# A hybrid decoder layer on one core: which engine issues the bias, decay, memory and copy transfers, how the second feed-forward is cut, and how its block C22 is summed

## The chip, the core and the metric

The kernel runs on one core of a Trainium2 chip. A core has five engines, each with its own instruction queue that it works through in order: TensorE (PE, matmuls and transposes), VectorE (DVE), ScalarE (ACT), GpSimd (POOL) and SyncE (SP, which only issues transfers). A DMA can be issued from SP, ACT or POOL; in the profile these issues stand on three transfer queues, q1 (from SP), q10 (from ACT) and q0 (from POOL, called software_dynamic there), and all three run on the same 16 DMA engines. The metric is the device time of one execution in microseconds.

## The reference, cut to what matters

One decoder layer on x (512 tokens, 1024 features, float32): a feed-forward, a mixer with two groups of heads, a cross-attention into a fixed memory of 256 rows, and a second feed-forward.

```python
x = x + 0.5 * swiglu(rms_norm(x, norm_ffn1_w), ffn1_w_in, ffn1_w_out)
x = x + hybrid_mixer(rms_norm(x, norm_mix_w), ...)
x = x + memory_cross_attention(rms_norm(x, norm_cross_w), rms_norm(mem, norm_mem_w), w_cq, w_ck, w_cv, w_co)
x = x + 0.5 * swiglu(rms_norm(x, norm_ffn2_w), ffn2_w_in, ffn2_w_out)
return rms_norm(x, norm_final_w)

def swiglu(h, w_in, w_out):                       # 1024 -> 2 x 2816 -> 1024
    gate, up = jnp.split(h @ w_in, 2, axis=-1)
    return (jax.nn.silu(gate) * up) @ w_out
...
logits = logits + bias[None, :, None]             # mixer: one bias row per head and distance
...
seg = la_cum[:, :, :, None] - la_cum[:, :, None, :]   # mixer: 16 scan heads, chunks of 128
decay = jnp.exp(jnp.where(causal, seg, -jnp.inf))
...
k = (mem_n @ w_ck); v = (mem_n @ w_cv)            # cross-attention, 4 heads
```

## The kernel before

Every float32 matrix product is made of three TensorE passes: each operand is split into a high part (wh, an ACT copy, line 153) and a low part (wl, a DVE subtraction, line 154), and high x high, high x low and low x high are summed in PSUM. A weight tile comes from DRAM into `wr` (six buffers, SP issues the load: `load_w` line 172, `raw_w` line 244, `fetch` line 1154) and is split into `wh` and `wl` (three buffers each).

The order is written out by hand through the class `Order`: a list of dense generators (projections) and chains (attention heads, scan groups, memory tiles, copies), which are woven together by an estimated TensorE time `od.t`. The program order that comes out is kept exactly for SP and POOL (`manual_schedule` of these two); the instructions of PE, DVE and ACT are put in order by the compiler's scheduler, with program order as priority. From then on every engine works through its own list in order and waits at each instruction for its semaphores. `with behind(ins)` puts an instruction after the named ones on the same engine.

What the change touches:

- **Bias.** `queries_keys` (line 671 on) makes q and k of one of eight attention heads and fetches `bias` (128 x 512, 256 KB) from `rel_z` in DRAM, line 676, issued by POOL. `head` reads it in `scores` (DVE, line 697, output `ec`).
- **Decay rows.** `decays` (line 813 on) broadcasts 4 x 128 numbers of `cum_d` to 128 partitions, two DMAs of 256 KB per call, line 819, issued by POOL, into the single buffers `gate` and `th`. The first calls stand in `steps` behind the write of `cum_d` (line 648); each later call stands in `group` behind the matmuls `py` that read the old rows.
- **Memory tiles.** `memory_tile` (line 934 on) loads an eighth of the memory. `memory_norm` and the first `memory_prep` (feed-forward 1, `early`) use SP and fetch all eight at the start. The second `memory_prep`, spawned by the last `out_attn` (line 768), fetches each tile by POOL just before its split into `hm` (lines 157 and 158); `memory_values` (tiles `pcv`) reads these.
- **Copies and adds.** Second feed-forward weights are block matrices in a scheme with seven products in place of eight. `block_sums_in_dram` prepares sums of weight blocks in DRAM beside the mixer: a copy (line 1138, issued by ACT, behind the last weight split) and, four jobs later, an accumulating DMA (line 1142, issued by POOL). There are 46 such jobs.
- **Thirds.** Each feed-forward's 22 tiles of hidden width go through in parts `THIRDS` of 8, 8 and 6: `ffn_quads` makes them two at a time, `out_blocks` applies the output matrix. The last part ends in `at_last`, whose ACT and DVE order is by hand: four products (`e_ps[0]`, `e_ps[1]`, `b_ps[0]`, `b_ps[1]`), after each an `update` of x, `norm` and `store`.
- **C22.** In `out_blocks` the block C22 = P5 - (b) is made by keeping a copy of `e_ps` in `p5` (ACT, line 1206), subtracting `b_ps` (DVE, line 1218, `c22`) and adding the result to x (`update`, DVE, line 1182).

Of the kernel before, what the change touches and what calls it, by code (L numbers as in the profile page):

```python
# [11 lines left out]
F32 = mybir.dt.float32  # L12
R32 = mybir.dt.float32r
AF = mybir.ActivationFunctionType
# [3 lines left out]
P = 128  # L18
# [5 lines left out]
EPS = 1e-6  # L24

NPLAIN = 6
THIRDS = ((0, 8), (8, 8), (16, 6))
NUM_BUCKETS = 32
MAX_DISTANCE = 128
RW = 640  # L30
# [68 lines left out]
def body(tc, a, dbg=None):  # L99
# [420 lines left out]
    def beside(ti):  # L520
        if ti == 1:
            od.spawn(prepare())
            od.spawn(memory_norm())
        elif ti == 2:
            od.spawn(memory_prep(hm, True))

    def fin1(o):
        st_mix.add(x[o])
# [142 lines left out]
    def queries_keys(hd):  # L671
        pq = acc("pq")
        yield from proj(pq, load_w(a["wq"][hd]), h)
        q = split("q", pq, -1.0)
        bias = s2("bias")
        nc.gpsimd.dma_start(bias, bass.AP(rel_z.tensor, rel_z.offset + hd * P * (RW + 1) + P - 1, [[RW, P], [1, T]]))
        pk = acc("pk")
        yield from proj(pk, load_w(a["wk"][hd]), h)
        kq = split("k", pk)
        od.spawn(head(hd, q, kq, bias), W["h0"])  # L680
# [84 lines left out]

    def out_attn(hg, o0, o1, prep=False):
        if prep:
            od.spawn(memory_prep(hm2, False), 0.0)
        yield lambda: all(y is not None for y in ya[4 * hg : 4 * hg + 4])
        heads = ya[4 * hg : 4 * hg + 4]  # L770
        for o in range(o0, o1):
            po = acc("pm")
            yield from proj(po, load_w(a["woa"][hg, o], 4 * P), heads)
            V.tensor_tensor(x[o], x[o], po, ALU.add)
        if o1 == KT:
            ya[4 * hg : 4 * hg + 4] = [None] * 4
# [36 lines left out]
    def decays(g, j):  # L813

        rows_of[g, j], both = [], s4(("gate", "th")[j])
        for hh in range(2):
            r = both[:, 2 * hh : 2 * hh + 2].rearrange("p a (b c) -> p (a b) c", c=P)
            hd = 4 * g + 2 * j + hh
            nc.gpsimd.dma_start(r, bass.AP(cum_d.tensor, cum_d.offset + hd * P, [[0, P], [16 * P, 4], [1, P]]))
            rows_of[g, j].append(r)  # L820

    def group(g, bt, ct, xs, zs):
# [108 lines left out]
    st_mem = Stat(MEM)  # L931
    ck, cv = [], []

    def memory_tile(k, queue):
        mk = s2("mem", shape=(P, MEM))
        queue.dma_start(mk, a["memT"][k])
        return mk

    def memory_norm():
        mem = [memory_tile(k, nc.sync) for k in range(KT)]  # L940
        for mk in mem:
            yield 2.0
            with behind(recent):
                st_mem.add(mk)
        yield 3.0
        yield from st_mem.finish(6.0)

    def memory_prep(dst, early):
        mem = [memory_tile(k, nc.sync) for k in range(KT)] if early else []
        for k in range(KT):  # L950
            mk = mem[k] if early else memory_tile(k, G)
            with behind(recent):
                dst.append(split("hm", mk, par[:, C_MEM + k : C_MEM + k + 1], True))
            yield 2.0
# [164 lines left out]


    isum = [[dram.tile([P, D], F32, name=f"isum{g}{t}") for t in range(2)] for g in range(NF // 2)]
    wsum = [[dram.tile([P, nf // 2 * T], F32, name=f"wsum{c}{t}") for t in range(4)] for c, (_, nf) in enumerate(THIRDS)]

    def block_sums_in_dram():
        jobs = []
        for c, (f0, nf) in enumerate(THIRDS):
            gs = range(f0 // 2, (f0 + nf) // 2)
            jobs += [(isum[g][0], a["f2q"][g][0], a["f2q"][g][1]) for g in gs]
            jobs += [(isum[g][1], a["f2q"][g][2], isum[g][0]) for g in gs]
            blocks, sums = a[f"f2b{c}"], wsum[c]  # L1130
            for t, (to, more) in enumerate(((blocks[B12], blocks[B11]), (blocks[B12], blocks[B22]), (blocks[B22], sums[0]), (blocks[B21], sums[2]))):
                for k in range(0, nf // 2 * T, D):
                    ks = slice(k, min(k + D, nf // 2 * T))
                    jobs.append((sums[t][:, ks], to[:, ks], more[:, ks]))
        for n in range(len(jobs) + LEAD):
            if n < len(jobs):
                with behind([i for i in recent if i.engine == mybir.EngineType.Activation]):
                    S.dma_start(jobs[n][0], jobs[n][1])
                yield 5.0
            if n >= LEAD:  # L1140
                to, _, more = jobs[n - LEAD]
                G.dma_start(to, more, accum_op=ALU.add, max_dma_last_dim=4 * D)
                yield 9.0

    def out_blocks(c, g, col4, last):


        blocks = a[f"f2b{c}"]
# [29 lines left out]
                for t in range(2):  # L1178
                    yield from some(ps[t], w, which, part, t, first)

        def update(tb, half_, src):
            V.scalar_tensor_tensor(x[4 * half_ + tb], src, col4[:, tb : tb + 1], x[4 * half_ + tb], ALU.mult, ALU.add)
            if last is not None:
                last[0](tb, half_)

        bank = [acc, aux]
# [11 lines left out]
                        yield  # L1198
        for m in both:
            yield from m  # L1200
        p5, u2 = [], []
        for t in range(2):
            S.activation(b_ps[t], a_ps[t], AF.Copy)
        for t in range(2):
            p5.append(s2("p5"))
            S.activation(p5[t], e_ps[t], AF.Copy)
        yield from product(b_ps, sums[2], S2)
        for t in range(2):
            u2.append(s2("u2"))
# [4 lines left out]
            update(t, 0, a_ps[t])  # L1214
        yield from product(b_ps, sums[1], S3)
        for t in range(2):
            c22 = s2("c22")
            V.tensor_tensor(c22, p5[t], b_ps[t], ALU.subtract)
            update(t + 2, 1, c22)
        if last is None:  # L1220
            yield from product(e_ps, blocks[B22], S4)
            for t in range(2):
# [28 lines left out]

    def ffn2():
        wq, in_sums = iter(a["f2q"]), iter(isum)
        col4, gain = None, []

        sq, root = {}, {}

        def norm(tb, n):

            xt, ss, junk = x[4 * n + tb], small("fss", 1), s2("junk")  # L1260
            S.activation(junk, xt, AF.Square, accum_out=ss)
            v = small("fv", 1, bufs=6)
            if tb not in sq:
                V.tensor_scalar(v, ss, 1.0 / D, EPS, ALU.mult, ALU.add)
            else:
                V.scalar_tensor_tensor(v, ss, 1.0 / D, sq[tb], ALU.mult, ALU.add)
            V.tensor_tensor(xt, xt, gain[n], ALU.mult)
            if tb not in sq:
                sq[tb] = v
                return  # L1270
            root[tb] = small("frr", 1)
            G.tensor_tensor(root[tb], v, mhalf[:, 0:1], ALU.pow)

        def store(tb):
            rr = root[tb]
            S.activation(x[tb], x[tb], AF.Copy, scale=rr)
            nc.sync.dma_start(a["out"][tb][:, :T], x[tb])
            if tb < 3:
                S.activation(x[4 + tb], x[4 + tb], AF.Copy, scale=rr)
            else:  # L1280
                V.tensor_scalar(x[4 + tb], x[4 + tb], rr, None, ALU.mult)
            (nc.sync if tb < 3 else S).dma_start(a["out"][tb][:, T:], x[4 + tb])

        for c, (_, nf) in enumerate(THIRDS):
            g = []
            yield from ffn_quads(xs_2, wq, st_2, nf // 2, block_tiles(g, nf // 2), BY_BLOCK, in_sums, c == 0)
            if c == 0:
                col4 = small("col4", 4, bufs=1)
                V.tensor_scalar(col4, st_2.col, 0.25, None, ALU.mult)
            at_end = c == len(THIRDS) - 1  # L1290
            if at_end:
                for n in range(2):
                    gain.append(s2("gain"))
                    G.dma_start(gain[n], a["final"][n].partition_broadcast(P))
            yield from out_blocks(c, g, col4, (norm, store) if at_end else None)

    od.add(turn(1))
    od.add(ffn2())
# [16 lines left out]
def layout(i):  # L1315
# [10 lines left out]
    for n, s in (("1", "ffn1"), ("2", "ffn2")):  # L1326
        wi = tiles(i[f"{s}_w_in"][0]).reshape(2 * NF, P, KT // 2, 2, P)
        f0 = NPLAIN if n == "1" else 0

        quads = [  # L1330
            np.stack([wi[u + f : u + f + 2, :, :, k].transpose(1, 0, 2, 3).reshape(P, D) for k in range(2) for u in (NF, 0)])
            for f in range(f0, NF, 2)
        ]
        d[f"f{n}q"] = np.stack(quads)
        if n == "1":
            d["f1i"] = wi.reshape(2, NF, P, D)[:, 2:NPLAIN].swapaxes(0, 1).copy()
        wo = i[f"{s}_w_out"][0]
        for t, (f0, nf) in enumerate(THIRDS):
            part = wo[f0 * P : (f0 + nf) * P]
            if n == "1":  # L1340
                d[f"f1o{t}"] = tiles(part)
            else:

                part = part.reshape(nf // 2, 2, P, 2, T).transpose(1, 3, 2, 0, 4)
                d[f"f2b{t}"] = np.ascontiguousarray(part).reshape(4, P, nf // 2 * T)
# [44 lines left out]
```

## Time and profile before

| | us |
|---|---|
| median of 3 runs | 1348.46 (1346.11 to 1348.67) |
| the profiled execution | 1348.15 |
| its span, first to last instruction | 1346.4 |
| DVE busy | 973.4 |
| ACT busy | 669.0 |
| POOL busy | 131.1 |
| moved by q1 (SP) / q0 (POOL) / q10 (ACT) | 150.30 / 47.79 / 23.33 MB |

The profile names a tile by its name without buffer numbers and an instruction by output <- inputs. Two names are cut short: `p` is `p5`, `c` is `c22`. A row of the timeline gives start, duration, engine, line, operation and, in brackets, how long the engine had been idle before it and what released it. A row with SPq, ACTq or POOL and DMA_DIRECT2D is the issue of a transfer, not the transfer; the time to landing stands beside it in the view of DMA issues. A row of the windows gives for each engine the busy time, then the granted TensorE clock (1.00 is full speed), the busy share of the DMA engines and GB/s.

### The profile page before, as it was taken

The page shows a single profiled execution, that of the slowest core. Times are in us where ns is not written, and L with a number is a line of the kernel's source. Part 1 is how long each engine was busy: PE and PEld are TensorE (multiplying, and loading weights), DVE is VectorE, ACT ScalarE, POOL GpSimd, SP SyncE. Part 2 cuts the span into 40 slices and gives each one's busy share as a digit, 9 for nine tenths or more (in the row PEclk, how much of TensorE's full clock was granted, in tenths as well). Part 3 has the DMA queues.
Part 4 walks back from the last instruction along what each step waited for, and adds up shares of the span by engine and source line. Part 5 has one row for each costly group of instructions (what it writes and reads, how often), then busy time and mean ns, then how long its engine had stood idle before and what let it go on. Part 6 is the DMA issues. An engine that isn't in the chain of part 4 may idle for free.

```text
span 1346.4 us, 20042 instructions
## 1 busy us (share of the span) xinstructions
PE 1312.3 (97%) x7769; PEld 1140.0 (85%) x7769; DVE 973.4 (72%) x1535; ACT 669.0 (50%) x1127; POOL 131.1 (10%) x155
## 2 busy tenths in 40 slices
PE   9999999999999899999999979999999999999996
PEld 7898998799887678877788867888889989998994
DVE  6875778487886476657867757656678876987786
ACT  6442445154544365336654536434455654655555
POOL 0000010000011110210103131020001100000001
PEclk9999999999999899999999989999999999999998
DMA  7434576455484734884359676675247866666653
GB/s 268 115 121 125 141 202 236 117 151 163 147 271 85 197 78 104 185 253 118 94 153 192 130 174 205 189 193 157 71 141 212 221 209 186 180 184 194 182 166 109
DMA packets 65695, 222.71 MB, mean 165 GB/s; under 512 B 8424, under 2 KB 10960, under 8 KB 65248
## 3 DMA queue, kind: packets, MB, share of 16 engines
q1 hardware_dynamic: 47088, 150.30, 34.3%
q0 software_dynamic: 14208, 47.79, 20.7%
q10 hardware_dynamic: 4304, 23.33, 5.3%
q8 instruction: 61, 1.00, 0.3%
q14 instruction: 34, 0.28, 0.1%
HBM read 219.24 MB, written 50.91 MB: 201 GB/s over the span
## 4 chain that ended last, share of the span: by engine, by line
PE 71%; issue 18%; DMA 4%; DVE 3%; POOL 2%; ACT 1%; POOLq 0%; SPq 0%; ACTq 0%; DVEq 0%
PE qb L238 10%; PE po L144 7%; PE qa L238 7%; PE qe L238 7%; PE pxbc L144 6%; PE pm L144 6%; PE pcq L144 3%; PE ob L1172 3%; PE pz L144 2%; PE oa L1172 2%; PE oe L1172 2%; PE pa L144 2%; PE pv L144 2%; PE pg L144 2%; PE pu L144 2%
## 5 line engine op out<-in xcount | busy, mean ns | idle before, releaser
L153 ACT ACTIVATE wh<-wr 128x1024 fp32r<-128x1024 f32 (+2 forms) x311 | 317.3, 1021 | 385.6 <-PE po L144 56.7
L154 DVE TENSOR_TENSOR wl<-wr,wh 128x1024 fp32r<-128x1024 f32 (+2 forms) x311 | 365.7, 1177 | 119.4 <-ACT wh L153 117.5
L144 PE MATMUL po<-gh,wh 128*128 128x512 f32 x176 | 68.9, 392 | 0.0
L144 PE MATMUL po<-gl,wh 128*128 128x512 f32 x176 | 68.5, 390 | 0.0
L144 PE MATMUL po<-gh,wl 128*128 128x512 f32 x176 | 68.4, 389 | 0.0
L238 PE MATMUL qa<-hmh,wl 128*128 128x256 f32 x216 | 61.2, 283 | 0.1
L238 PE MATMUL qa<-hml,wh 128*128 128x256 f32 x216 | 61.1, 283 | 0.0
L238 PE MATMUL qa<-hmh,wh 128*128 128x256 f32 x216 | 61.1, 283 | 0.0
L698 ACT ACTIVATE ec<-ec,mn 128x512 f32<-128x512 f32 (+3 forms) x64 | 35.4, 555 | 36.0 <-DVE mn L697 36.0
L144 PE MATMUL pxbc<-hnh,wh 128*128 128x512 f32 x128 | 52.4, 409 | 0.0
L144 PE MATMUL pxbc<-hnh,wl 128*128 128x512 f32 x128 | 50.4, 393 | 0.0
L144 PE MATMUL pxbc<-hnl,wh 128*128 128x512 f32 x128 | 50.1, 391 | 0.0
L238 PE MATMUL qe<-s31h,wh 128*128 128x256 f32 x152 | 43.7, 288 | 1.7 <-ACT wh L153 1.7
L238 PE MATMUL qe<-s31h,wl 128*128 128x256 f32 x152 | 43.9, 289 | 0.8 <-DVE wl L154 0.8
L504 DVE TENSOR_TENSOR upd<-po,row 128x512 f32<-128x512 f32 x24 | 16.6, 691 | 38.1 <-PE po L144 37.8
L238 PE MATMUL qe<-s31l,wh 128*128 128x256 f32 x152 | 43.5, 286 | 0.0
L238 PE MATMUL qb<-s24h,wh 128*128 128x256 f32 x152 | 43.0, 283 | 0.0
L238 PE MATMUL qb<-s31h,wl 128*128 128x256 f32 x152 | 43.0, 283 | 0.0
L238 PE MATMUL qe<-s24h,wh 128*128 128x256 f32 x152 | 43.0, 283 | 0.0
L238 PE MATMUL qe<-s24l,wh 128*128 128x256 f32 x152 | 43.0, 283 | 0.0
L238 PE MATMUL qe<-s24h,wl 128*128 128x256 f32 x152 | 43.0, 283 | 0.0
L238 PE MATMUL qb<-hmh,wh 128*128 128x256 f32 x152 | 43.0, 283 | 0.0
(448 smaller groups left out, 4103.8 us busy)
## 6 DMA issues: line engine op xcount, KB each, us to landing
wr<-in_f2q SPq DMA_DIRECT2D x44, 512.0 KB, 4.4
wr<-in_f1q SPq DMA_DIRECT2D x40, 512.0 KB, 4.1
isum<-in_f2q ACTq DMA_DIRECT2D x22, 512.0 KB, 5.3
wr<-isum SPq DMA_DIRECT2D x22, 512.0 KB, 4.4
wsum<-in_f2b ACTq DMA_DIRECT2D x20, 512.0 KB, 5.1
wr<-wsum SPq DMA_DIRECT2D x20, 512.0 KB, 4.6
wr<-in_f1q POOLq DMA_DIRECT2D x16, 512.0 KB, 6.3
wr<-in_f1o SPq DMA_DIRECT2D x16, 512.0 KB, 4.7
```

What stands on the lines that cost most here:

```text
L144: nc.tensor.matmul(out, w, x, start=start, stop=stop)
L153: S.activation(hi, src, AF.Copy),
L154: V.tensor_tensor(lo, src, hi.bitcast(F32), ALU.subtract),
L238: nc.tensor.matmul(out, a_[:, wc], b_, start=first and f == 0 and kp == 0 and j == 0, stop=kp == n - 1 and j == 2, skip_group_check=True)
L504: V.tensor_tensor(upd, po, row4, ALU.mult)
L698: S.activation(ec[:, :n], ec[:, :n], AF.Exp, bias=mn, scale=-1.0, accum_out=sm[c][:, i : i + 1])
L1172: nc.tensor.matmul(ps, a_[:, ts], b_[:, ws], start=first and k == 0 and j == 0, stop=k == n - 1 and j == 2, skip_group_check=True)
```

## The change

```diff
 THIRDS = ((0, 8), (8, 8), (16, 6))
+THIRDS2 = ((0, 6), (6, 8), (14, 8))
...
-            od.spawn(memory_prep(hm, True))
+            od.spawn(memory_prep(hm))
...
-        nc.gpsimd.dma_start(bias, bass.AP(rel_z.tensor, ...))
+        S.dma_start(bias, bass.AP(rel_z.tensor, ...))
...
-            od.spawn(memory_prep(hm2, False), 0.0)
+            od.spawn(memory_prep(hm2), 0.0)
...
-            nc.gpsimd.dma_start(r, bass.AP(cum_d.tensor, ...))
+            S.dma_start(r, bass.AP(cum_d.tensor, ...))
...
-    def memory_prep(dst, early):
-        mem = [memory_tile(k, nc.sync) for k in range(KT)] if early else []
-        for k in range(KT):
-            mk = mem[k] if early else memory_tile(k, G)
+    def memory_prep(dst):
+        mem = [memory_tile(k) for k in range(KT)]
+        for k, mk in enumerate(mem):
...
-                with behind([i for i in recent if i.engine == mybir.EngineType.Activation]):
-                    S.dma_start(jobs[n][0], jobs[n][1])
+                nc.sync.dma_start(jobs[n][0], jobs[n][1])
...
-        def update(tb, half_, src):
-            V.scalar_tensor_tensor(x[4 * half_ + tb], src, col4[:, tb : tb + 1], x[4 * half_ + tb], ALU.mult, ALU.add)
-            if last is not None:
+        def update(tb, half_, src, sign=1, done=True):
+            col = (col4 if sign > 0 else ncol4)[:, tb : tb + 1]
+            V.scalar_tensor_tensor(x[4 * half_ + tb], src, col, x[4 * half_ + tb], ALU.mult, ALU.add)
+            if last is not None and done:
                 last[0](tb, half_)
...
         for t in range(2):
-            p5.append(s2("p5"))
-            S.activation(p5[t], e_ps[t], AF.Copy)
+            update(t + 2, 1, e_ps[t], 1, False)
         yield from product(b_ps, sums[2], S2)
...
         for t in range(2):
-            c22 = s2("c22")
-            V.tensor_tensor(c22, p5[t], b_ps[t], ALU.subtract)
-            update(t + 2, 1, c22)
+            update(t + 2, 1, b_ps[t], -1)
...
+                ncol4 = small("ncol4", 4, bufs=1)
+                V.tensor_scalar(ncol4, st_2.col, -0.25, None, ALU.mult)
```

ScalarE issues the 8 bias and 16 decay transfers in place of GpSimd. SyncE issues all memory tiles, the eight of a call at its start, and the 46 copies. GpSimd keeps the 46 accumulating transfers and its other small work. The second feed-forward (`ffn2`, `block_sums_in_dram`, `wsum` and the layout of its output weights) uses `THIRDS2`, parts of 6, 8 and 8 tiles; the first keeps 8, 8, 6. C22 is added to x in two steps, first `e_ps` times the column and later `b_ps` times its negative, so that `p5` and `c22` go.

More of the change, by code (lines that the diff above doesn't have):

```diff
@@ L675, in queries_keys @@
         bias = s2("bias")
-        nc.gpsimd.dma_start(bias, bass.AP(rel_z.tensor, rel_z.offset + hd * P * (RW + 1) + P - 1, [[RW, P], [1, T]]))
+        S.dma_start(bias, bass.AP(rel_z.tensor, rel_z.offset + hd * P * (RW + 1) + P - 1, [[RW, P], [1, T]]))
         pk = acc("pk")
@@ L818, in decays @@
             hd = 4 * g + 2 * j + hh
-            nc.gpsimd.dma_start(r, bass.AP(cum_d.tensor, cum_d.offset + hd * P, [[0, P], [16 * P, 4], [1, P]]))
+            S.dma_start(r, bass.AP(cum_d.tensor, cum_d.offset + hd * P, [[0, P], [16 * P, 4], [1, P]]))
             rows_of[g, j].append(r)
@@ L932, in body, with memory_tile @@
     ck, cv = [], []
-    def memory_tile(k, queue):
+    def memory_tile(k):
         mk = s2("mem", shape=(P, MEM))
-        queue.dma_start(mk, a["memT"][k])
+        nc.sync.dma_start(mk, a["memT"][k])
         return mk
     def memory_norm():
-        mem = [memory_tile(k, nc.sync) for k in range(KT)]
+        mem = [memory_tile(k) for k in range(KT)]
         for mk in mem:
@@ L946, in memory_norm @@
         yield from st_mem.finish(6.0)
-    def memory_prep(dst, early):
-        mem = [memory_tile(k, nc.sync) for k in range(KT)] if early else []
-        for k in range(KT):
-            mk = mem[k] if early else memory_tile(k, G)
+    def memory_prep(dst):
+        mem = [memory_tile(k) for k in range(KT)]
+        for k, mk in enumerate(mem):
             with behind(recent):
@@ L1121, in body @@
     isum = [[dram.tile([P, D], F32, name=f"isum{g}{t}") for t in range(2)] for g in range(NF // 2)]
-    wsum = [[dram.tile([P, nf // 2 * T], F32, name=f"wsum{c}{t}") for t in range(4)] for c, (_, nf) in enumerate(THIRDS)]
+    wsum = [[dram.tile([P, nf // 2 * T], F32, name=f"wsum{c}{t}") for t in range(4)] for c, (_, nf) in enumerate(THIRDS2)]
     def block_sums_in_dram():
         jobs = []
-        for c, (f0, nf) in enumerate(THIRDS):
+        for c, (f0, nf) in enumerate(THIRDS2):
             gs = range(f0 // 2, (f0 + nf) // 2)
@@ L1143, in block_sums_in_dram, with out_blocks @@
                 yield 9.0
-    def out_blocks(c, g, col4, last):
+    def out_blocks(c, g, col4, ncol4, last):
         blocks = a[f"f2b{c}"]
@@ L1200, in out_blocks @@
             yield from m
-        p5, u2 = [], []
+        u2 = []
         for t in range(2):
@@ L1253, in ffn2 @@
         wq, in_sums = iter(a["f2q"]), iter(isum)
-        col4, gain = None, []
+        col4, ncol4, gain = None, None, []
         sq, root = {}, {}
@@ L1282, in store @@
             (nc.sync if tb < 3 else S).dma_start(a["out"][tb][:, T:], x[4 + tb])
-        for c, (_, nf) in enumerate(THIRDS):
+        for c, (_, nf) in enumerate(THIRDS2):
             g = []
@@ L1288, in ffn2 @@
                 col4 = small("col4", 4, bufs=1)
+                ncol4 = small("ncol4", 4, bufs=1)
                 V.tensor_scalar(col4, st_2.col, 0.25, None, ALU.mult)
-            at_end = c == len(THIRDS) - 1
+                V.tensor_scalar(ncol4, st_2.col, -0.25, None, ALU.mult)
+            at_end = c == len(THIRDS2) - 1
             if at_end:
@@ L1294, in ffn2 @@
                     G.dma_start(gain[n], a["final"][n].partition_broadcast(P))
-            yield from out_blocks(c, g, col4, (norm, store) if at_end else None)
+            yield from out_blocks(c, g, col4, ncol4, (norm, store) if at_end else None)
     od.add(turn(1))
@@ L1337, in layout @@
         wo = i[f"{s}_w_out"][0]
-        for t, (f0, nf) in enumerate(THIRDS):
+        for t, (f0, nf) in enumerate(THIRDS if n == "1" else THIRDS2):
             part = wo[f0 * P : (f0 + nf) * P]
```

## The prediction

> **What bounds the kernel now.** I read the page's first part, then TensorE's own waits, then windows around each wait. The span and the engines:
>
> ```profile
> span 1346.4 us, 20042 instructions
> PE 1312.3 (97%) x7769; PEld 1140.0 (85%) x7769; DVE 973.4 (72%) x1535; ACT 669.0 (50%) x1127; POOL 131.1 (10%) x155
> ```
>
> TensorE works for 1312.3 of 1346.4 us. The change alters no matmul (22 tiles of width go through the same products in either cut), so all there is to win lies in the 34.1 us in which it stands, and in matmuls that run at a lower clock. Its longest waits (who waited, for whom, total, times, longest):
>
> ```profile
> PE pf L144 <- ACT st L862: 5.3, 1, 5.3
> PE pt L148 <- DVE mn L697: 2.6, 1, 2.6
> ```
>
> Few and single. Windows around the first two places, and the tail:
>
> ```profile
> core 0: us, PE busy (x) PEld busy (x) DVE busy (x) ACT busy (x) POOL busy (x), PEclk, DMA share, GB/s
> 457.00:462.00 5.00, 1.13 (x8) 0.73 (x8) 3.71 (x11) 3.10 (x7) 0.00 (x0) 0.88 0.61 145
> 462.00:468.00 6.00, 6.00 (x20) 4.31 (x20) 5.25 (x16) 3.83 (x11) 0.00 (x0) 0.54 0.41 123
> 795.00:803.00 8.00, 1.24 (x5) 0.60 (x3) 2.63 (x6) 2.81 (x5) 1.09 (x2) 0.73 0.74 200
> 803.00:809.00 6.00, 6.00 (x17) 4.85 (x18) 5.97 (x10) 4.89 (x12) 0.00 (x0) 0.51 0.13 38
> 1334.00:1346.40 12.40, 0.00 (x0) 0.00 (x0) 4.10 (x9) 5.17 (x11) 2.79 (x3) 0.66 0.45 169
> ```
>
> A stall costs twice. At 457 TensorE stands for 5.00 - 1.13 = 3.87 us, and in the next 6 us it is busy throughout at a mean granted clock of 0.54, which loses 6.00 x 0.46 = 2.76 us: **6.6 us**. At 795 it stands for 8.00 - 1.24 = 6.76 us and then loses 6.00 x 0.49 = 2.94 us: **9.7 us**. The tail, 12.4 us without a matmul, is the third place.
>
> **What causes the two stalls.** The first, in the timelines of POOL and DVE:
>
> ```profile
> 438.00 1.03 POOL L756 TENSOR_TENSOR rr<-ev,mhalf 128x4 f32<-128x4 f32 x1 [9.36 <-DVE ev L754]
> 439.00 0.93 POOL L1142 DMA_DIRECT2D isum<-in_f2q  x1
> 439.64 0.88 POOL L676 DMA_DIRECT2D bias<-rel_z  x1
> ```
>
> ```profile
> 457.25 0.69 DVE L697 CUSTOM_DVE_ANT_0 ec<-ps,bias 128x512 f32<-128x512 f32 x1 [9.26 <-DMA bias<-rel_z]
> ```
>
> POOL stood at line 756, let an add go first and the bias behind it; DVE then waited 9.26 us for the bias, and TensorE, which needs DVE's `mn`, stood for 3.87 of them. So TensorE has about 9.26 - 3.87 = 5.4 us of cover there. The second, in the timelines of POOL and ACT:
>
> ```profile
> 785.56 0.93 POOL L1142 DMA_DIRECT2D wsum<-in_f2b  x1
> 786.20 0.89 POOL L936 DMA_DIRECT2D mem<-in_memT  x1
> ```
>
> ```profile
> 799.83 0.51 ACT L157 ACTIVATE hm<-mem,par 128x256 fp32r<-128x256 f32 x1 [10.35 <-DMA mem<-in_memT]
> ```
>
> The first memory tile is issued behind an add as well and lands 799.8 - 786.2 = 13.6 us later. ACT stands in its list at the split `hm` for 10.35 us; behind it is the copy `st` that TensorE's `pf` needs. The tile is wanted much later, by `pcv`: the stall comes from the order in ACT's queue.
>
> **The change, part by part.**
>
> *Memory tiles to SP, eight at once.* Prices of both ways, over the whole run (issues, KB each, median us to landing):
>
> ```profile
> mem<-in_memT SPq DMA_DIRECT2D x16, 128.0 KB, 4.5
> ...
> mem<-in_memT POOLq DMA_DIRECT2D x8, 128.0 KB, 11.1
> ```
>
> SP issues in program order and as far ahead as its six `wr` buffers allow. The new tiles stand between the loads of the last `woa` and the first `wcv`. The view of the load line puts the last `woa` issue at 749.2 us (last number but the count):
>
> ```profile
> L172 SPq DMA_DIRECT2D wr<-in_woa x16: 327/328/328, 468.6 to 749.2; - x16
> ...
> DMA to landing us min/median/max: 2.5/4.7/27.7
> ```
>
> Issued from about 749 on, eight tiles of 4.5 us, even one after the other, land by 785, before ACT reaches `hm` at 799.83 - 10.35 = 789.5, and even the longest landing of that line, 27.7 us, would do for a tile (777). The stall goes: **-9.7 us**. What is late next? On DVE, busy for only 2.63 of the 8 us, the low halves of `hm` have room. If SP must wait for free small buffers, the term falls to 0.
>
> *Bias to ACT.* The row that speaks for it comes from the view of DMA issues between 436 and 458 us:
>
> ```profile
> bias<-rel_z POOLq DMA_DIRECT2D x2, 256.0 KB, 19.4
> ...
> wr<-in_wxbc SPq DMA_DIRECT2D x1, 512.0 KB, 17.2
> wsum<-in_f2b ACTq DMA_DIRECT2D x1, 512.0 KB, 9.8
> ```
>
> In this crowded stretch POOL's transfers of 256 KB took 19.4 us, one of twice the size on ACT's queue 9.8. On ACT the bias is no longer behind adds, but it is behind the first four decay transfers, which also move there. I take 9.8 us. Issued near 440.5, it lands near 450; DVE was free at 457.25 - 9.26 = 448, so it waits 2 to 3 us, within the 5.4 us of cover: **-6.6 us**. Bounds: 0, if it lands later than about 457 as now, and -6.6.
>
> [...]
>
> *Decay rows to ACT.* Off the path: no compute engine waits for them now. They leave POOL's queue, ahead of `rr` and the adds. In ACT's list they add waits, for the write of `cum_d` (issued by POOL) and six times for `py`. Queued behind such an issue are ACT's weight splits `wh`, and for those TensorE waits, with three buffers of splits as cover. How long POOL stood at these two kinds of issue:
>
> ```profile
>   PE ps L144: 58.6, 2
> ```
>
> ```profile
>   PE py L144: 99.2, 6
> ```
>
> POOL reached them far too early, since its list holds little else. ACT reaches them through its own work, which the scheduler has put in an order by its estimate. Bounds per issue: 0, and the mean of the longer kind, 58.6 / 2 = 29.3 us, less the cover. The nearest row for an engine with a full list is ACT's own, 10.35 us at `hm`; it took a transfer queued behind another. I take 0, because `py` and `ps` are matmuls that end before ACT's next inputs come, and hold the rest for a rival.
>
> *Copies to SP; issue costs.* An issue on ACT (ns, in the middle the median):
>
> ```profile
> L1138 ACTq DMA_DIRECT2D wsum<-in_f2b x24: 497/498/610, 445.3 to 991.2; - x24
> ```
>
> At 0.50 us per issue ACT loses 46 x 0.50 = 23 us and gains 24 x 0.50 = 12; at the 0.33 us of the load rows SP gains 46 x 0.33 = 15 us in 1346. Neither is near its limit. On SP's queue a copy stands ahead of weight loads and delays them by its transfer. No TensorE wait is due to a load even where landing took 17.2 us, since loads run up to six buffers ahead; cost 0, bounded above by one stall of the second kind, 9.7. POOL keeps the adds, and its waits no longer hold anything else.
>
> *Thirds of 6, 8, 8 and C22 in two steps.* Inside, the boundaries now have no stall, and a part of three pairs exists already. Per part two ACT copies and no DVE operation net go (two subtractions go, two updates come). The tail is where it counts. Rows of TensorE, ACT and DVE there, then the subtraction that goes:
>
> ```profile
> 1324.68 0.39 PE L1172 MATMUL oe<-wh,s24h 128*128 128x512 f32 x1
> ...
> 1326.72 0.39 PE L1172 MATMUL oe<-wh,s24h 128*128 128x512 f32 x1
> ...
> 1332.93 0.63 PE L1172 MATMUL ob<-wl,gh 128*128 128x512 f32 x2
> ```
>
> ```profile
> 1332.61 0.72 ACT L1276 ACTIVATE x<-x,frr 128x512 f32<-128x512 f32 x1 [0.79 <-POOL frr L1272]
> ...
> 1342.23 0.72 ACT L1276 ACTIVATE x<-x,frr 128x512 f32<-128x512 f32 x1 [1.31 <-POOL frr L1272]
> ```
>
> ```profile
> 1338.46 0.74 DVE L1182 SCALAR_TENSOR_TENSOR x<-ob,col,x 128x512 f32<-128x512 f32 x1
> ```
>
> ```profile
> L1218 DVE TENSOR_TENSOR c<-p,ob 128x512 f32<-128x512 f32 x6 | 4.1, 684 | 0.1
> ```
>
> The tail is not TensorE's: the last matmul ends at 1333.56, yet the last `update` starts only at 1338.46. Four `store` steps follow each other (1342.23 - 1332.61) / 3 = 3.2 us apart, through ACT, DVE and POOL's `frr`, and the first of them hangs on `e_ps[0]`, the first of four products of nine matmuls. Nine took 1326.72 - 1324.68 = 2.04 us. With eight tiles each product has twelve, 2.72 us; counted back from the same end of TensorE's work, `e_ps[0]` is complete 3 x 0.68 = 2.04 us earlier, and the chain with it. Two subtractions of 0.68 us leave DVE's list there; the second pair of splits doubles in width and takes about as much back. I take **-2.0**, bounds 0 (ACT too full to start earlier) and -4.6 (the last `update` starts right at TensorE's end plus 0.3 us, 1333.9 for 1338.5).
>
> **Sum**, against the profiled execution of 1348.15 us (span 1346.4 and 1.75 around it; the median of the runs is 0.3 above): 1348.15 - 9.7 - 6.6 - 2.0 = 1329.85, forecast **1330.0 us**.
>
> **Rivals.**
> 1. *The bias stays late* (same DMA engines, decay rows ahead of it). For it: the DMA engines' load and the 17.2 us load; against it: no add ahead, and 9.8 us. Time 1329.85 + 6.6 = 1336.5. Chance 0.15.
> 2. *The memory tiles come late all the same*, because SP must wait for eight small buffers of 16 while the scan groups hold some: the change then does not do what it says. Against it: SP is some 40 us ahead. 1329.85 + 9.7 = 1339.5. Chance 0.07.
> 3. *ACT stops at an issue, and the time is slower than before.* Place: the bias of a fourth head, whose buffer a `ps` matmul must free; POOL stood there 29.3 us on the mean. Price, if ACT stands as long: 29.3 less 5.4 of cover, 23.9, and 2.8 at the low clock, 26.7: 1356.5. It decides from a stop of about 5.4 + 18.3 - 2.8 = 21 us on. For it: ACT's list is in order, and a split behind it feeds TensorE. Against it: `ps` itself needs ACT's splits. Chance 0.12; a shorter stop that costs 9 to 16 us, 1339 to 1346: 0.08.
> 4. *Other places take back all that is won*, within 0.2%: 0.05.
>
> **How the numbers follow.** Forecast 1326 to 1333: 0.50; below that (smaller gaps go too, full bound of the tail): 0.03; rivals as above. About 0.2%, 2.7 us, is what a measurement can tell from no change. Faster: 0.50 + 0.03 + 0.15 + 0.07 + 0.08 = 0.83; same 0.05; slower 0.12. The range from 1325 (tail at -4.6 and some luck) to 1345 holds the forecast, the first two rivals and most of the short stop, about 0.8.
>
> **What would show it.** TensorE's waits without `pf` behind ACT `st` and without the 2.6 us behind `mn`; granted clock 1.00 in both windows; bias landing in about 10 us on ACTq; memory tiles issued on SPq more than 20 us before `hm`, and no wait of ACT for `mem`; the first tail `store` about 2 us nearer to TensorE's last products and the last matmul still before the last `update`. It would be wrong if ACT's waits show issues held by `ps`, `py` or `cum_d` for more than 5 us with a TensorE wait on `wh` behind them, or if TensorE waits for a weight load on SP.

## The result, and the profile after

| | before | after |
|---|---|---|
| median (lowest to highest, runs) | 1347.14 (1344.76 to 1348.67, 6) | **1336.84** (1334.78 to 1339.30, 6) |
| ratio, 95% interval | | **0.9925** [0.9909, 0.9942] |
| the profiled execution | 1348.15 | 1334.78 |

The change makes the kernel 10.3 us faster; 1330.0 was forecast. The profiled execution of after is its fastest one, so the two traces differ by 13.4 us. The head of the page, and TensorE's waits of after (who waited, for whom, total, times, longest):

```profile
span 1333.0 us, 20031 instructions
...
PE 1308.7 (98%) x7769; PEld 1136.9 (85%) x7769; DVE 974.5 (73%) x1536; ACT 666.5 (50%) x1121; POOL 107.2 (8%) x123
```

```profile
PE nrow L146 <- DVE ndiag L365: 2.3, 3, 1.6
PE pf L146 <- DVE st L872: 1.7, 1, 1.7
...
PE pck L146 <- DVE wl L156: 1.2, 1, 1.2
```

`pf` no longer waits 5.3 us for ACT's `st`, nor `pt` 2.6 us for `mn`. `pck` now waits for DVE, which is new, and `nrow` waits longer for DVE than before (2.3 us in all and 1.6 at most, from 1.3 and 0.7). Windows of after around a new place, the two old ones and the tail:

```profile
378.00:382.00 4.00, 2.22 (x16) 1.81 (x16) 4.00 (x6) 2.21 (x3) 3.05 (x1) 1.00 0.06 24
382.00:388.00 6.00, 5.02 (x26) 4.36 (x25) 5.62 (x12) 3.55 (x7) 0.91 (x2) 0.72 0.96 261
455.00:460.00 5.00, 5.00 (x25) 3.71 (x25) 2.14 (x7) 2.46 (x6) 0.00 (x0) 1.00 0.96 261
460.00:466.00 6.00, 6.00 (x36) 4.47 (x35) 5.25 (x18) 3.62 (x11) 0.00 (x0) 1.00 0.54 178
786.00:794.00 8.00, 4.15 (x18) 2.81 (x17) 7.39 (x15) 5.60 (x12) 0.00 (x0) 1.00 0.99 234
794.00:800.00 6.00, 6.00 (x28) 4.64 (x27) 4.09 (x8) 6.00 (x15) 0.00 (x0) 1.00 1.05 426
1322.44:1333.00 10.56, 0.00 (x0) 0.00 (x0) 2.67 (x6) 3.30 (x8) 1.85 (x2) 0.74 0.40 149
```

At 455 TensorE is now busy throughout at full clock. At 786 it still stands for 8.00 - 4.15 = 3.85 us, without a low clock behind. At 378 it stands for 1.78 us, where it stood for 0.60 before, and at 382 the clock falls. The tail is 10.56 us long, from 12.8.

The stretches below run from the start of one TensorE row to that of another, the same two in every trace, so that each difference belongs to its stretch. e1 is the best version found below.

| stretch (times of before) | before | after | e1 | forecast |
|---|---|---|---|---|
| `pck` to `pv`, 361.8 to 403.1 | 41.3 | +3.97 | 0.0 | 0 |
| first heads, 431.1 to 484.7 | 53.6 | -6.07 | -6.48 | -6.6 |
| 484.7 to 518.8 | 34.1 | -1.29 | -1.25 | 0 |
| last groups' `pxbc`, 709.4 to 774.2 | 64.9 | +0.95 | -0.05 | 0 |
| last scan group to `pcv`, 788.2 to 836.6 | 48.5 | -7.49 | -6.31 | -9.7 |
| last matmul to the end | 13.2 | -2.25 | -3.61 | -2.0 |
| all else | | -1.2 | -0.4 | 0 |
| span | 1346.4 | -13.4 | -18.1 | -18.3 |

The sum looks nearly right term by term. The runs show that the bias term is not what it looks like.

### The profile page after: what moved, and what is told of

Read it like the earlier page. It is cut to its first block, busy times and chain, and to the rows that moved or that the text cites. A ratio compares the mean times of both kernels' runs of the same rounds, so it can differ in the third digit from the quotient of the medians.

```text
span 1333.0 us, 20031 instructions
## 1 busy us (share of the span) xinstructions
PE 1308.7 (98%) x7769; PEld 1136.9 (85%) x7769; DVE 974.5 (73%) x1536; ACT 666.5 (50%) x1121; POOL 107.2 (8%) x123
## 3 DMA queue, kind: packets, MB, share of 16 engines
q0 software_dynamic: 11904, 40.45, 16.6%
## 4 chain that ended last, share of the span: by engine, by line
PE 91%; DVE 4%; ACT 1%; DMA 1%; issue 1%; POOL 0%; POOLq 0%; SPq 0%; ACTq 0%; DVEq 0%
PE qb L240 12%; PE po L146 10%; PE pm L146 10%; PE qa L240 8%; PE qe L240 8%; PE pxbc L146 6%; PE pcq L146 3%; PE pv L146 3%; PE ob L1172 3%; PE pz L146 3%; PE pq L146 3%; PE pk L146 2%; PE oa L1172 2%; PE oe L1172 2%; PE pa L146 2%; PE pcv L146 2%
## 5 line engine op out<-in xcount | busy, mean ns | idle before, releaser
L506 DVE TENSOR_TENSOR upd<-po,row 128x512 f32<-128x512 f32 x24 | 16.6, 691 | 38.1 <-PE po L146 37.8
L240 PE MATMUL qb<-s24h,wl 128*128 128x256 f32 x152 | 43.1, 284 | 0.0
L240 PE MATMUL qb<-hml,wh 128*128 128x256 f32 x152 | 43.0, 283 | 0.0
L240 PE MATMUL qb<-hmh,wl 128*128 128x256 f32 x152 | 43.0, 283 | 0.0
```

The lines of the kernel that those rows point to most:

```text
L240: nc.tensor.matmul(out, a_[:, wc], b_, start=first and f == 0 and kp == 0 and j == 0, stop=kp == n - 1 and j == 2, skip_group_check=True)
L506: V.tensor_tensor(upd, po, row4, ALU.mult)
```

## The experiments

The runs of one kernel differ by 1.5 to 9 us, so single edits are read from their stretches in the trace, and the medians decide only where they are far apart. Two stretches move by up to 2 us even where an edit touches nothing in them: p1 is 1.50 us shorter than before in the first heads, p4 1.95 in the last scan group. The other stretches of the table agree within 0.05 us in the runs whose edits don't reach them.

| run | median (range, runs) | ratio to before, 95% |
|---|---|---|
| u1 decays back on GpSimd | 1334.93 (1332.41 to 1337.96, 4) | 0.9920 [0.9892, 0.9949] |
| u2 copies back on ScalarE | 1336.63 (1331.75 to 1337.87, 4) | 0.9919 [0.9891, 0.9947] |
| u3 both back | 1334.50 (1332.59 to 1335.10, 4) | 0.9907 [0.9885, 0.9930] |
| p1 memory alone | 1340.22 (1338.15 to 1342.71, 7) | 0.9951 [0.9934, 0.9968] |
| p2 bias alone | 1344.53 (1340.56 to 1346.22, 10) | 0.9974 [0.9958, 0.9990] |
| p3 parts alone | 1336.04 (1334.39 to 1337.72, 4) | 0.9911 [0.9884, 0.9939] |
| p4 C22 alone | 1346.23 (1345.44 to 1349.48, 10) | 0.9991 [0.9979, 1.0004] |
| d1 first decays later in the list | 1340.53 (1337.66 to 1341.51, 5) | 0.9945 [0.9924, 0.9966] |
| e1 first decays behind the bias rows | **1329.84** (1328.82 to 1331.08, 4) | **0.9872** [0.9857, 0.9886] |
| e2 u3 without the memory's move | 1336.26 (1335.21 to 1336.67, 4) | 0.9918 [0.9903, 0.9933] |
| e4 before, sums two places ahead | 1345.86 (1340.84 to 1349.42, 10) | 0.9988 [0.9973, 1.0003] |
| f1 before, first decays as in e1 | 1353.32 (1351.49 to 1356.13, 7) | 1.0043 [1.0028, 1.0059] |

### u1, u2, u3: the decays and the copies back where they were

```diff
-            S.dma_start(r, bass.AP(cum_d.tensor, ...))         # u1, u3
+            nc.gpsimd.dma_start(r, bass.AP(cum_d.tensor, ...))
-                nc.sync.dma_start(jobs[n][0], jobs[n][1])      # u2, u3
+                with behind([i for i in recent if i.engine == mybir.EngineType.Activation]):
+                    S.dma_start(jobs[n][0], jobs[n][1])
```

> Changed kernel with the decay rows issued by GpSimd again, all else as changed. Theory A (SyncE's stream was held at the memory tiles by the decay transfers of ScalarE, since a transfer on these two queues waits for the one eight before it): the memory tiles are issued by 760 us rather than up to 781, the next out-projection weights before 775 rather than 782, and the TensorE gaps of 3.8 us between 787 and 793 fall to 1.5 or less; time 2 to 4 us under the changed kernel. Rival B (SyncE was held because small buffers were not free): the tiles go out as late as before, gaps stay at 3.8. The new gaps at 379 to 386 us stay in both.

> Changed kernel with the 46 copies issued by ScalarE again, all else as changed. Theory A (with the copies on SyncE the scheduler puts the weight splits behind the splits of the normed x in the lists of VectorE and ScalarE, which makes the TensorE gaps of 2.8 us and the low clock at 379 to 386): those gaps fall to about 0.6 us, as before the change, and the first values matmul starts about 4 us earlier against the same matmul of the changed kernel. Rival B (the bias or the memory tiles cause it): they stay. The hold of SyncE at the memory tiles stays in both theories.

> Changed kernel with decay rows on GpSimd and copies on ScalarE again; bias, memory tiles, parts and C22 as changed. If both theories hold, both places are mended: 1334.8 - 4 - 2.5 = about 1328 us in the profiled execution. If the two places are not independent, or GpSimd's queue gets late again with decay rows and adds, no faster than the better of the two single ones.

With the copies on ScalarE again, the stretch 361.8 to 403.1 is as before (-0.01 in u3, +3.97 in after). DVE's timeline in after, and then in u2:

```profile
377.30 0.68 DVE L156 TENSOR_TENSOR hnl<-hf,hnh 128x512 fp32r<-128x512 f32 x1
377.90 0.74 DVE L405 SCALAR_TENSOR_TENSOR hf<-x,par,row 128x512 f32<-128x512 f32 x1
378.57 0.68 DVE L156 TENSOR_TENSOR hnl<-hf,hnh 128x512 fp32r<-128x512 f32 x1
379.17 0.74 DVE L405 SCALAR_TENSOR_TENSOR hf<-x,par,row 128x512 f32<-128x512 f32 x1
379.83 1.22 DVE L156 TENSOR_TENSOR wl<-wr,wh 128x1024 fp32r<-128x1024 f32 x1
```

```profile
375.32 1.22 DVE L156 TENSOR_TENSOR wl<-wr,wh 128x1024 fp32r<-128x1024 f32 x1
...
380.91 1.21 DVE L156 TENSOR_TENSOR wl<-wr,wh 128x1024 fp32r<-128x1024 f32 x1
```

The window of u2 there, where TensorE stands for 0.60 us as in before:

```profile
378.00:382.00 4.00, 3.40 (x26) 2.96 (x25) 4.00 (x7) 3.26 (x5) 3.97 (x2) 1.00 1.01 398
```

The same operations stand in another order. In after the weight split `wl`, for which TensorE's `pck` waits, comes behind a row of `hf` and `hnl` that TensorE first reads at 386; DVE is busy for all of 378 to 382 in both. Moving a copy's issue off ScalarE changed the order that the scheduler gives ScalarE and DVE, and that costs the 4 us. TensorE waits there for DVE and ACT, not for a transfer. The total shows none of these 4 us: u2 is at 1336.63, after at 1336.84. What u2 wins at 380 it misses at 457: in the first heads u2 and u3 gain only 1.31 and 1.49 us on before, after 6.07. So the two places are not independent, and u3, at 1334.50, missed the 1328 that was expected.

The decays on ScalarE cost 0.95 us (after) and 0.59 us (u2) between 709 and 774, where u1 and u3 show -0.03 and 0.01. They also cost 1.3 us at the end: in after, where ScalarE issues the decays, the closing rows of the trace stand behind a DRAIN of GpSimd that lasts 5.67 us, to 1332.23, 1.4 us past the landing of the last store; in before, where GpSimd issues them, it lasts 3.91 us and is over 0.3 us ahead of that landing. From the last store's issue to the end of the span it is 4.7 us in after, 3.5 in u1 and 3.4 in u3. Why the DRAIN is longer no run shows. The decays also hold SP. SP's waits at the memory tiles in after:

```profile
SPq L938 <- DMA gate<-cum_d: 25.3, 2, 21.9
```

That is one wait of 21.9 us for a transfer that SP did not issue. But with the decays on GpSimd the gaps of TensorE at 788 to 793 are the same (1.58, 1.69 and 0.59 us in u1), so the hold is free, and theory A of u1, which had these gaps shrink, is wrong.

### p1, p2, p3, p4: one part of the change at a time

Each on the kernel before, with the hunks of the change that belong to it (in full above):

```diff
+        mem = [memory_tile(k, nc.sync) for k in range(KT)]      # p1, in every memory_prep
+        for k, mk in enumerate(mem):
...
-        nc.gpsimd.dma_start(bias, ...)                           # p2
+        S.dma_start(bias, ...)
...
+THIRDS2 = ((0, 6), (6, 8), (14, 8))                              # p3, second feed-forward
...
+            update(t + 2, 1, e_ps[t], 1, False)                  # p4, in place of p5 and c22
...
+            update(t + 2, 1, b_ps[t], -1)
```

> Kernel before with only the memory tiles moved to SyncE, eight at once. Theory A: without decay rows on ScalarE nothing holds SyncE, so the stall at 795 us goes whole: the stretch from the last gate matmul to the end of the values matmuls of the cross-attention shrinks by about 10 us, time about 1338.5. Rival B (buffers): the tiles are held as in the changed kernel and the stretch shrinks by 7.5 us or less.

> The kernel before with one edit: the bias rows are issued by ScalarE. The prediction's step: the row lands after about 9.8 us instead of 17.5, so the wait of `em` for `bias` (8.59 us on DVE) and the gap of 2.64 us with the low clock behind it go, 6.6 us in 431 to 485. Rival (the same DMA engines are filled by the first four decay broadcasts, whichever queue carries the bias): landing 14 to 17 us, DVE still waits 7 to 9 us for `bias`, the gap of 2.6 us in `pt` stays, the stage is at most 1.5 us shorter. About 1341.5 by the first, 1346 to 1348 by the second.

> The kernel before with the second feed-forward's parts of 6, 8 and 8 tiles and nothing else. The shift of the last results comes from the larger last part or from C22's shorter chain, and this run parts them. If the parts carry it, the closing stretch from the last matmul to the end is 2 to 3.6 us shorter and the run 1344 to 1346; if C22 carries it, the closing stretch is within 0.7 us of before and the run within 0.1%. Total matmul work is the same, so no other stage should differ by over 0.5 us.

> The kernel before with only C22 added in two steps: ScalarE's two copies `p5` and DVE's two subtractions go, two early DVE updates come in their place. The chain behind the last products loses two DVE operations on [128 x 512] of 0.6 to 0.8 us each, so the closing stretch is 1.2 to 1.6 us shorter if those subtractions lie on it, and nothing if the last two stores wait only for `x[2]`, `x[3]`. Between 1345.5 and 1348.

**p1.** ACT's timeline shows `hm` without a wait, and `st` right behind it; TensorE's waits the next late thing:

```profile
787.58 0.50 ACT L157 ACTIVATE hm<-mem,par 128x256 fp32r<-128x256 f32 x1
787.98 0.37 ACT L862 ACTIVATE st<-pst 128x256 f32<-128x256 f32 x1
```

```profile
789.15 0.71 PE L144 MATMUL nrow<-ndiag,ones_r 128*128 128x512 f32 x2 [1.58 <-DVE ndiag L363]
792.63 0.49 PE L144 MATMUL pf<-th,st 128*128 128x128 f32 x2 [1.69 <-DVE st L870]
794.16 0.50 PE L144 MATMUL pm<-yah,wl 128*128 128x512 f32 x1 [0.57 <-DVE wl L154]
```

The stretch is 6.33 us shorter (3.91 to the first `pcv` and 2.42 behind it), not 9.7. TensorE's rows now wait for DVE, 3.84 us in all. The size is that of rival B, but its cause, tiles held by buffers, is not there: `hm` waits for no tile.

**p2.** On ScalarE's queue the row took as long as on GpSimd's. From the views of line 676 in p2 (who waited; landing) and, with the same columns, in after:

```profile
  DVE ec L697: 8.1, 1
...
DMA to landing us min/median/max: 2.6/3.9/16.6
```

```profile
L678 ACTq DMA_DIRECT2D bias<-rel_z x8: 326/338/357, 397.8 to 634.7; - x8
...
  DVE ec L699: 4.2, 1
...
DMA to landing us min/median/max: 2.6/3.6/12.6
```

The longest landing is that of the row of this stretch: 16.6 us in p2, 12.6 us in after, 17.5 us before. The gap of 2.64 us at `pt` stays in p2 and the stretch is 1.53 us shorter. That is rival 1. Even the 1.53 us are not the edit's: p1, which leaves the bias alone, is 1.50 us shorter there; the mean granted clock of the stretch is 0.97 in p2, for 0.94 in before. What the queue does show is in the next stretch, 484.7 to 518.8: p2 is 0.86 us shorter, every other run with the bias on ScalarE 1.24 to 1.29, p1 0.00. The profiled execution of p2, 1346.20, is one of the slowest of its ten, so the median gain of 2.6 us is not all in this trace.

**p3.** This run was far outside both expectations: 1336.04, nearly the whole change. Its tail is 2.98 us shorter, as the first expectation had it, but 2.94 us went between 431 and 485 and 5.09 us between 788 and 837, in stages that the edit doesn't name. The memory tiles in p3's view of DMA issues, and the first split in ACT's timeline:

```profile
mem<-in_memT POOLq DMA_DIRECT2D x8, 128.0 KB, 7.1
```

```profile
792.73 0.51 ACT L158 ACTIVATE hm<-mem,par 128x256 fp32r<-128x256 f32 x1 [6.62 <-DMA mem<-in_memT]
```

The tiles still come from GpSimd's queue, but land in 7.1 us instead of 11.1; ACT waits 6.62 us for the first instead of 10.35, and `pf` behind it 1.6 us instead of 5.3. What differs at that time is what else is moved: with a first part of six tiles the list of block sums has 14 entries for that part instead of 16, the half-wide sums come first instead of last, and everything behind stands two places ahead.

**p4.** The closing stretch is 0.45 us shorter, below the 1.2 to 1.6 expected from the subtractions. The time is the same within the interval.

### e2 and e4: memory without the move, and the sums two places ahead

```diff
+        jobs = jobs[:14] + jobs[16:32] + jobs[14:16] + jobs[32:]      # e4, on the kernel before
         for n in range(len(jobs) + LEAD):
```

```diff
-    def memory_prep(dst):                                            # e2, on u3: as before
+    def memory_prep(dst, early):
+        mem = [memory_tile(k, nc.sync) for k in range(KT)] if early else []
+        for k in range(KT):
+            mk = mem[k] if early else memory_tile(k, G)
```

> The kernel of u3_both_back with the memory tiles as before: four ahead on SyncE's queue or on GpSimd's, where they were. It tells what moving the memory is worth once the parts are 6, 8 and 8. If the move and the parts are substitutes (both only bring the tiles' landing ahead of `hm`), this run is 0.5 to 2 us slower than 1334.5, as the stages of p3_parts_alone (5.09 of 6.31 us) add up. If the move is worth on its own what p1_memory_alone showed, 6.3 us, it is at 1340 or above.

> The kernel before with one edit: the last two of the first part's block sums in DRAM are made after the second part's, so that from the fifteenth on every copy and addition comes two places earlier, as it does with parts of 6, 8 and 8. If the gain of p3_parts_alone between 785 and 837 comes from which block sums run beside the memory tiles, the gap of 4.98 us in `pf` shrinks to 1.6 us here too and that stage is 3 to 5 us shorter, with 431 to 485 and the end as before: 1341.5 to 1345. If it comes from the shorter first part itself, nothing changes: 1346 to 1348.

e2 came as the first theory expected: 1.8 us slower than u3 by the medians. Moving the memory and the new parts are **substitutes**: alone they are worth 6.9 and 11.1 us, but once the parts are there the move adds about 2. e4 shows a part of why. In its timelines ACT waits for the tile, and TensorE for ACT:

```profile
795.77 0.51 ACT L157 ACTIVATE hm<-mem,par 128x256 fp32r<-128x256 f32 x1 [7.56 <-DMA mem<-in_memT]
```

```profile
796.60 0.58 PE L144 MATMUL pf<-th,st 128*128 128x128 f32 x2 [2.52 <-ACT st L862]
```

The gap of `pf` is 2.52 us, where it was 5.32 in before and 4.54 to 5.98 in p2, p4 and f1, which leave the order alone; the stretch is 3.29 us shorter. That is through the order of the sums alone, but not to p3's 1.58, and the median, 1345.86, misses the expected range by 0.9 us with an interval that includes no change. So the order of the block sums moves this stall; how much of p3's 5.1 us it makes in a mean run stays open, and so does the 1.4 us by which p3 beats p1 and p2 between 431 and 485.

### d1, e1, f1: what makes the bias late

d1, on u3: the first four decay broadcasts are put 40 us later in the hand-written order. e1, on u3, and f1, on the kernel before: the cumulative sum itself is written only behind the third head's first scores, by a true dependence.

```diff
+            yield 40.0                      # d1, ahead of the first decays in steps()
...
+    def first_decays(mn):                   # e1 and f1, called in scores() for hd == 2, i == 3
+        z = small("zmn", 1)
+        V.tensor_scalar(z, mn, 0.0, None, ALU.mult)
+        ct_2 = s2("ct_2", shape=(64, P))
+        V.tensor_scalar(ct_2, ct_of[0], z[:64], None, ALU.add)
+        nc.gpsimd.dma_start(cum_d, ct_2)
+        for j in range(2):
+            decays(0, j)
```

> The changed kernel with decay rows on GpSimd and copies on ScalarE again (the kernel of u3_both_back), and the first four decay broadcasts (256 KB each, in pieces of 512 bytes) are issued some 40 us later than the cumulative sum they read; the rows are first used some 60 us after that. If these four broadcasts fill the DMA engines and so hold the bias row, the row of 444 lands in 3 to 6 us instead of 16.6, DVE's wait of 8.1 us for it goes, and 431 to 485 is 3 to 5 us shorter than in u3_both_back: about 1330. If the bias is late for another reason (its own 512 rows, the queue, the three additions on GpSimd's queue), it still lands after 12 us or more and the time is that of u3_both_back, 1334.5 within 0.2%.

> The kernel of u3_both_back with the cumulative sum written to DRAM, and with it the first four decay broadcasts, only after the third head's first scores (two small DVE operations carry the dependence), that is at about 478 instead of 422; the rows are first read at 529. In d1_first_decays_later the same four landed on the second bias row (20.2 us) instead of the first (3.5 us). If these broadcasts are what holds the bias, all three rows now land in at most 6 us, no wait of DVE for `bias` over 1 us and no gap of PE over 1 us stay between 431 and 485, and with the low clock gone too that stage is about 4 us shorter than in u3_both_back: 1330 to 1331. If the block sums' copies and additions hold it as well, the first row still takes 8 us or more and the time is within 0.15% of 1334.5. If the broadcasts now land after 529, ScalarE waits for them and the time is above 1336.

> The kernel before with one edit, that of e1_decays_after_bias: the first four decay broadcasts go out after the third head's first scores. The bias rows stay on GpSimd's queue. With p2_bias_alone (the queue changed, the broadcasts where they were) it parts the two causes. If the broadcasts alone hold the bias, its rows land in at most 8 us on GpSimd's queue too, the gaps of 1.57 and 2.64 us and the low clock between 431 and 485 go, and that stage is 5.5 to 6.6 us shorter than before: about 1341. If ScalarE's queue is needed as well, the rows still take over 10 us, a gap of PE over 1 us stays, and the run is at 1344 to 1347.

**d1** missed its time but shows the mechanism. The timeline of its issues:

```profile
439.75 0.33 ACTq L679 DMA_DIRECT2D bias<-rel_z  x1
440.55 2.19 POOL L822 DMA_DIRECT2D gate<-cum_d  x2
442.14 2.08 POOL L822 DMA_DIRECT2D th<-cum_d  x2
...
452.24 0.33 ACTq L679 DMA_DIRECT2D bias<-rel_z  x1
```

GpSimd's list holds little else, so a later place in it is no wait: the broadcasts went out at 440.55, not 462. The row issued 0.8 us ahead of them landed in 3.5 us, the next one, 10 us behind them, in 20.2 us, and DVE waited 8.0 us for it one head later.

**e1** did what was expected, and its time is 0.2 us below the expected range. Line 686 (the bias issue), and the two windows of before:

```profile
DMA to landing us min/median/max: 2.5/3.2/10.4
```

```profile
455.00:460.00 5.00, 5.00 (x27) 3.83 (x26) 4.24 (x14) 3.36 (x11) 0.00 (x0) 1.00 0.33 109
460.00:466.00 6.00, 6.00 (x35) 4.31 (x34) 5.18 (x17) 3.15 (x10) 0.00 (x0) 1.00 0.16 46
```

The three rows of this stretch landed in 3.2, 2.5 and 3.1 us, TensorE is busy throughout, and the stretch is 6.48 us shorter than before. At 1329.84 us this is the fastest version, 7.0 us (half a per cent) below the change itself; 4.7 of these are against u3, from which only the delayed broadcasts part it.

**f1** gave the expected stretch and a wrong total. From 431 to 485 it gained 6.60 us with the rows still on GpSimd's queue (6.0 and 10.7 us to landing). Then, in the timeline of POOL and in that of DVE:

```profile
471.16 1.48 POOL L829 DMA_DIRECT2D th<-cum_d  x2
472.64 0.93 POOL L1152 DMA_DIRECT2D isum<-isum  x1
473.23 0.92 POOL L684 DMA_DIRECT2D bias<-rel_z  x1
```

```profile
494.82 0.69 DVE L705 CUSTOM_DVE_ANT_0 ec<-ps,bias 128x512 f32<-128x512 f32 x1 [11.65 <-DMA bias<-rel_z]
```

The row of the next head stands behind the delayed broadcasts on GpSimd and lands 21.5 us later; TensorE stands for 9.93 us and the stretch from 485 to 519 is 12.53 us longer. In e1 the same row goes out on ScalarE at 469.08, 0.9 us ahead of the first broadcast at 470.00. The delay alone (f1) and the queue alone (p2) each leave a row behind the broadcasts. Together they work here, but by a margin of 0.9 us: in d1 a row that was issued behind the broadcasts was late on ScalarE's queue too.

## Why the prediction was right where it was, and where not

1. **Bound and places: right.** The two stalls and the tail are where the time went, and a stop of TensorE cost the gap and, at 457 and 795 in before and at 378 in after, a stretch at a granted clock of 0.50 (6.8, 10.2 and 3.4 us). The three gaps at 786 to 793 in after brought none.
2. **Bias, -6.6: the size is reached, the mechanism failed.** The step that failed is "On ACT the bias is no longer behind adds", so "I take 9.8 us". The queue was not what mainly held it: the row took 16.6 us alone on ScalarE (p2) and 12.6 in after; with the broadcasts behind it, it takes 2.5 to 3.5 on ScalarE (d1, e1) and 6.0 and 10.7 on GpSimd (f1). Rival 1 was the true mechanism. The page of before gives the time on the three queues as shares of the same 16 DMA engines (q1 34.3, q0 20.7, q10 5.3%), and p2, which moved the rows from q0 to q10 and nothing else, has 16.6 us for 17.5. That after still gains 6.07 us there has another reason: the stall at 380 makes all compute 4 us later. DVE is free for the row at 456.81 - 4.19 = 452.6 in after and at 449.4 in p2 (8.07 us of wait until 457.43), while the row lands at about 457 in both. The 5.4 us of cover was right: a wait of 4.19 us stopped nothing, one of 8.07 stopped `pt` for 2.64. The gain at 457 and the loss at 380 are largely one exchange: over both, 361.8 to 484.7, after gains 2.11 us, u3 1.50, p2 1.53, p1, without the bias's move, 1.51, and e1 6.49. The total fell near rival 1's 1336.5, and that the forecast range holds it is in part luck: the bias's term gave nothing of its own there. Why the row lands no later in after than in p2, though the first broadcast (429.81 for 426.86) and the row (444.04 for 440.75) were issued 3 us later, was not tested.
3. **Memory tiles, -9.7: right mechanism, over-sized.** ACT's wait is gone in p1 and after. Alone it gives 6.33 us, since `nrow` (1.58), `pf` (1.69) and `pm` (0.57) then wait for DVE, which the prediction, looking at DVE's share of that window, had found free. What would remove these gaps was not tried. Rival 2 fell: SP was held up to 21.9 us, at no cost. Four tiles went out at 728.6 to 745.3, the other four only at 767.5 to 781.4, the last 5 us ahead of the first `hm` at 786.39 and not the 20 that the prediction asked for.
4. **Copies to SP, 0: wrong, +3.97.** The prediction looked for the price on SP's queue, where in after the 33 weight loads that were issued behind a copy still under way landed after 7.1 us in the median, the other 251 after 4.3 (by the trace's rows). It lay in the order of DVE's list, which no view of the kernel before could show. In the total the loss is not seen (u2), for the reason in point 2.
5. **Decays to ACT, 0: too low.** 0.6 to 0.95 us are lost in the last groups and 1.3 at the end, about 2 in all; the medians of after and u1 are 1.9 apart, with ranges that overlap. Rival 3's stop did not come in after: no wait of TensorE for `wh` is over 1.7 us. But its mechanism, a bias row stuck behind other work, is what made f1 slower, on GpSimd.
6. **Tail, -2.0: right mechanism, under-sized.** From the end of the last matmul to the last `store` on ACT it was 1342.23 - 1333.56 = 8.67 us. After, by the rows of ACT and TensorE:

```profile
1317.52 0.72 ACT L1274 ACTIVATE x<-x,frr 128x512 f32<-128x512 f32 x1 [0.31 <-POOL frr L1270]
...
1327.56 0.72 ACT L1274 ACTIVATE x<-x,frr 128x512 f32<-128x512 f32 x1 [1.31 <-POOL frr L1270]
```

```profile
1322.05 0.39 PE L1172 MATMUL ob<-wl,gh 128*128 128x512 f32 x1
```

   1327.56 - 1322.44 = 5.12 us: 3.55 less. The first `store` is 1322.44 - 1317.52 = 4.92 us ahead of the last matmul's end, where it was 0.95 ahead: 3.97 us earlier, for the 2.04 of the prediction. Of the 3.55 p3 gives 2.97 and p4 0.45, so the parts carry it. In after 1.3 us is lost again behind the last store (the stretch is 2.25 shorter, in u3 3.60), in GpSimd's longer DRAIN (5.67 us, 3.91 in before).
7. **Parts elsewhere, "Inside, the boundaries now have no stall": incomplete.** The cut also orders the block sums in DRAM, and with p3 that was worth more than the tail. Since it removes the same stall as the memory's move, the sum over the parts tried alone (6.9 + 2.6 + 11.1 + 0.9 us below 1347.14, 21.5) is twice what the change gives.

## What to carry to other kernels

When a small transfer lands late, look at everything that the DMA engines move at that time before changing its queue: four broadcasts of 256 KB in 512-byte pieces, which nothing needs for 100 us, made the urgent row four to six times slower here (12.6 us in after, 16.6 in p2, 17.5 in before, 3.2 in e1), and the cure here was to send them later by a true dependence, since a later place in a near-empty list was no wait (440.55 us in d1, for the 462 meant). Then see that the urgent transfer is issued ahead of it, on whichever queue. And after any edit of what an engine issues, compare the order of its neighbours' lists: here a moved issue cost 4 us at a place where no transfer was late.

## What the runs showed of the hardware

**Ahead of the tail the low clock came in multiples of 3.4 us.** Windows of before, cut at the changes of the granted clock (PEclk, the last figure but two):

```profile
460.80:467.60 6.80, 5.73 (x15) 4.12 (x17) 6.05 (x19) 4.11 (x12) 0.00 (x0) 0.50 0.50 137
467.60:474.00 6.40, 6.40 (x37) 4.58 (x39) 4.58 (x16) 3.37 (x11) 0.57 (x1) 1.00 0.27 85
798.70:808.90 10.20, 6.79 (x18) 5.39 (x19) 8.53 (x15) 7.60 (x16) 1.09 (x2) 0.50 0.30 86
```

It is 0.50 for 6.8 and 10.2 us here, for 3.4 us in after at 382 (0.50 from 382.0 to 385.4), for 3.4 us in p3 at both places (0.50) and, by an estimate from the windows of f1 (0.70 from 483 to 496, 0.51 from 496 to 502), for 13.7 us behind its gap of 9.93 us. So 3.4 us of it cost 1.7 us where TensorE is busy, an estimate from 3.4 x 0.50. The same gaps brought it or not: behind gaps of 1.67 and 0.76 us near 270 it is 0.51 in before (269.6 to 273.1) and 1.00 in after (268 to 276).

**SP's issues waited for ScalarE's transfers in this program.** In after SP stood at a memory tile until `gate<-cum_d`, which ScalarE had issued, was landed (the 21.9 us above). The semaphores that the trace of after gives for the transfers of SP (383) and ScalarE (25) are the same eight, in the program's order taken in turn, and at the last four memory tiles SP waited for the transfer eight places before, which was ScalarE's: each tile has that transfer's semaphore and went out within 0.1 us of its landing.

| ScalarE issued | landed | SP issued the tile |
|---|---|---|
| 759.67 | 767.47 | 767.53 |
| 760.08 | 771.27 | 771.35 |
| 770.08 | 777.63 | 777.65 |
| 770.48 | 781.28 | 781.35 |
